# Expert weight loads: five instead of three outstanding, and chunks that are contiguous in DRAM

## The chip, the cores and the metric

The kernel runs as one program on one core of a Trainium2 chip. The metric is the device time of one execution in microseconds (us), as the median of several runs. The engines of the core that matter here are TensorE (PE), VectorE (DVE), ScalarE (ACT), GpSimd (POOL) and SyncE (SP, which issues most of the transfers), and the 16 DMA engines that all transfers share.

## The reference, cut to what matters

One layer of a streaming encoder runs over 1088 tokens (1024 of a prompt and 64 of a sample) with a model width of 1024. Attention, a short convolution and their merge come first. The part that the change touches is the mixture of experts behind them:

```python
def expert_block(args):          # 32 experts, hidden width 256; each token goes to 2 of them
    xblk, eid = args
    a = xblk @ w1[eid]           # 1024 -> 256
    b = xblk @ w3[eid]           # 1024 -> 256
    return (jax.nn.silu(a) * b) @ w2[eid]   # 256 -> 1024
```

The weighted outputs of a token's two experts are added to the residual. A last step adds `sigmoid(RMSNorm(x) @ w_pg) * (p @ w_ple)`. All inputs are float32. Each expert has 1024 x 512 weights in w1 and w3 together and 256 x 1024 in w2, so 3.146 MB; the 32 experts are 100.7 MB.

## The kernel before, in words

**Precision.** A product of float32 matrices is made of three matmuls (`mm3`, L60 to L63): each operand is split into a high part (`hi`, a cast on ACT, L55) and the rest (`lo`, a subtraction on DVE, L58). So each weight chunk that arrives in SBUF as `eraw` is first cast to `weh` on ACT and then subtracted to `wel` on DVE, before TensorE can use it. That pair is `e_split`.

**The order of the stages.** Projections, heads and attention; the merge with the output projection and the routing, token tile by token tile; the experts; then the combination of the experts' outputs with the gate (`f_comb`, `f_tr`, `f_mm`).

**The experts.** They run one after the other, e = 0 to 31. The rows of an expert's tokens (at most 96) are fetched from DRAM with an indirect transfer on POOL (`gather`, L1280, into one of three buffers `xg`), transposed on TensorE (`x_tr`), multiplied with w1 and w3 (`w13_mm`, 24 matmuls), passed through the activation (`act_`), transposed again (`a_tr`) and multiplied with w2 (`w2_mm`, 12 matmuls). The result `y` is copied out of PSUM by ACT (L1333) and written to the DRAM tensor `Yd` with another indirect transfer on POOL (`scatter`, L1336), which also ends the expert's work. The second product of expert e runs among the matmuls of expert e + 1.

**The weights.** An expert's weights are six chunks of [128, 1024] float32, 512 KB each (4 of w1 and w3, 2 of w2). `e_load` (L900) loads them into slots of SBUF; there are slots for five experts (`EP`), so the load for expert e + 5 waits until the chunk of expert e in the same slot has been split. The chunks of the first six experts are requested in the stages before the experts, among the loads and stores of the merge; from then on `late(e)` requests those of expert e + 6. SP's program order is written out by hand in these stages (`manual_schedule`), as is POOL's in the expert stage; the order on PE, ACT and DVE in the expert stage is made by the scheduler, from a model of times of its own.

**The bound on the queue.** Every load of weights goes through `w_dma` (L892 to L898): the load is given a dependency on the load issued three before it, so SP does not issue it before that one has landed:

```python
        r = eng.dma_start(dst, src)
        if len(wdma) >= 3:
            tc.add_manual_dep(r.ins, wdma[-3].name,
```

The same queue carries what the last step needs: five loads for `p @ w_ple` (`pl_load`, tiles `plr`) and eight of `w_pg` (`wpg_load`, tiles `eraw` from `in_wpg_dram`), which are requested after the last expert's chunks.

**The layout in DRAM.** The host packs the weights as `we` of shape [32, 128, 6144]: for each expert and each of the 128 partitions, 6 x 1024 numbers in a row. Chunk j of expert e is the slice `we[e, :, 1024 * j : 1024 * j + 1024]`: 128 pieces of 4 KB that lie 24 KB apart.

**After the experts.** A loop on the chip (`For_i`, L1524) serves tokens beyond an expert's first 96 rows; its count is worked out on the chip and no instruction of its body is in the trace of this input. All engines meet at it. Then SP loads the rows for the combination (`f_x`, `f_y`, L1572 and L1583; the latter read `Yd`, which the scatters wrote).

Of the kernel before, what the change touches and what calls it, by code (L numbers as in the profile page):

```python
# [32 lines left out]
NOV = 22  # L33
NOROW = 2200.0
A2 = 2 * T


@with_exitstack
def body(ctx, tc, a):
# [10 lines left out]
    def opened(*args, **kw):  # L50
        st = ExitStack()
        return st, st.enter_context(pool(*args, **kw))
# [17 lines left out]
    def load(p, shape, src, tag, bufs):  # L70
        raw = p.tile(shape, F32, name=tag + "_r", tag=tag + "_r", bufs=bufs)
        nc.sync.dma_start(raw, src)
        return raw
# [30 lines left out]
    h2d = dram.tile([T, D], F32, name="h2d")  # L104
    Yd = dram.tile([A2, D], F32, name="Yd")

    psA, pb = opened("pb", bufs=8, space=PSUM)

    def bank():
        return pb.tile([128, 512], F32, name="bk", tag="bk")  # L110
# [16 lines left out]

    ws, wp = opened("win", bufs=2, side="right")

# [1 line left out]
    wraw = {}  # L131
    wsp = {}

# [60 lines left out]
            lo(zTl[:, ct, o:o + n], zf[:, o:o + n], zTh[:, ct, o:o + n])  # L194
        return f

# [1 line left out]
    xs_, xp = opened("xin")  # L198
    nc.scalar.dma_start(ident, a["ident"])
    grow = xp.tile([1, D], F32, name="grow")  # L200
# [130 lines left out]
    jobs = [("b", 0, 2)]  # L331
# [28 lines left out]
    for j, (kind, d, g) in enumerate(jobs):  # L360
# [9 lines left out]
        for ci, (o, n) in enumerate([c for c in CH if c[0] < TB] if kind in "ag" else CH):  # L370
# [5 lines left out]
            if ci == 0:  # L376
# [3 lines left out]
                if j >= len(jobs) - 8:  # L380
                    k = j - (len(jobs) - 8)
                    r = load(gs_["qp"], [128, 544], a["wqkv"][:, k], "wq", 2)
# [8 lines left out]
    ws.close()  # L391
    zs.close()

# [1 line left out]
    lat, lp = opened("lat", side="right")  # L395
    kpe = lp.tile([32, NK], F32, name="kpe")
    gcol = lp.tile([64, 2], F32, name="gcol")
# [176 lines left out]
                                in1=rs[:, :, None].to_broadcast([128, NH, 64]), op=OP.mult)  # L574
        nc.sync.dma_start(knd[i // 4][:, :, i % 4].rearrange("q p c -> p q c"), kn.rearrange("p (q t) c -> p q (t c)", t=2))

# [1 line left out]
    FCH = [c for c in CH if c[0] >= TB]  # L578
    fw, fps, psF = {}, {}, []

# [44 lines left out]
    for nm, n, dst in (("wuq", 768, wu), ("wukv", 1024, wk)):  # L625
        for k in range(2):
            r = up.tile([128, 1024], F32, name="wup_r", tag="wup_r", bufs=1)
# [54 lines left out]
    fill_n(4)  # L682
    psA.close()

# [1 line left out]
    hws.close()  # L686
    us.close()
    lat.close()
# [149 lines left out]
    for u in range(-3, NU + 1):  # L838
        if 0 <= u < NU:
            u_T(u)  # L840
        if u + 3 < NU:
            h3, i3 = UN[u + 3]
            first = u == -3 or UN[u + 2][0] != h3
# [16 lines left out]
        o = u_PV(u - 1) if u >= 1 else None  # L860
# [8 lines left out]
    hbs.close()  # L869
    psS.close()  # L870

# [1 line left out]
    psB, pb = opened("pb2", bufs=7, space=PSUM)  # L873
    pst, ptab = opened("ptab", space=PSUM)
    tab = ptab.tile([128, 64], F32, name="tab")
# [3 lines left out]
    def slot(j, shape, dt, name):  # L879
        return (fx if j < 24 else fx2[0]).tile(shape, dt, name=name, tag=f"fx{j}", bufs=1)  # L880
# [9 lines left out]
    wdma = []  # L890

    def w_dma(dst, src, eng=nc.sync):  # L892
        r = eng.dma_start(dst, src)
        if len(wdma) >= 3:
            tc.add_manual_dep(r.ins, wdma[-3].name,
                              mybir.DependencyInfo(mybir.DependencyClass.Sync, mybir.DependencyReason.DATA),
                              reason="bounded queue")
        wdma.append(r.ins)  # L898

    def e_load(e, js=range(6)):  # L900
        for j in js:
            r = slot(3 * EP[e % len(EP)][j // 3] + j % 3, [128, 1024], F32, "eraw")
            w_dma(r, a["we"][e, :, 1024 * j:1024 * j + 1024])
            eraw[e, j] = r

    ys, yp = opened("ya", bufs=2)
# [35 lines left out]
    gates = lgp.tile([128, 2, NT], F32, name="gates")  # L942
# [155 lines left out]
        nc.vector.scalar_tensor_tensor(out=lg[:n, i], in0=ps[:n, 0:36], scalar=rs_.pop(i)[:n], in1=brt[:n],  # L1098
                                       op0=OP.mult, op1=OP.add)

# [1 line left out]
    V_ = nc.vector  # L1102
    gdesc, edesc, rid, ovn = c1[:, 0:4], c1[:, 4:12], c1[:, 12:140], c1[:, 140:140 + NOV]
    val, tok4 = c2[:, 0], c2[:, 1:5].rearrange("p (k s) t -> p k s t", k=2)
# [72 lines left out]
    for i in range(6):  # L1177
        p = i - 1
# [92 lines left out]
    V_.tensor_scalar(out=idx[:CAP].rearrange("p s e -> p (s e)"), in0=tab[:CAP], scalar1=NOROW, scalar2=None, op0=OP.add)  # L1271
    xs2.close()

# [1 line left out]
    xgs_, xgp = opened("xg")  # L1275
    xT, ab, act, aT2, yy = {}, {}, {}, {}, {}
    xgs = [xgp.tile([128, D], F32, name=f"xg{j}", bufs=1) for j in range(3)]
# [57 lines left out]
    def scatter(buf, col):  # L1335
        nc.gpsimd.indirect_dma_start(out=Yd[:, :], out_offset=bass.IndirectOffsetOnAxis(ap=col, axis=0), in_=buf,  # L1336
                                     in_offset=None, bounds_check=A2 - 1, oob_is_err=False)

# [5 lines left out]
    e_load(5)  # L1344
    order.close()

# [1 line left out]
    eps_, ep = opened("moe", bufs=2)  # L1348
    x_tr(0, xgs[0], 0, ep, CAP)
    x_tr(0, xgs[0], 1, ep, CAP)  # L1350
# [161 lines left out]
    eps_.close()  # L1512
    xgs_.close()

# [1 line left out]
    ops_, op_ = opened("ovf")  # L1516
    order = ExitStack()
    order.enter_context(tc.manual_schedule(engines={ET.DVE, ET.Activation, ET.SP}))
# [5 lines left out]
    with tc.For_i(0, nov, 1) as i:  # L1524
        ev = nc.values_load(ovi[0:1, bass.ds(i + 1, 1)], engines=(mybir.EngineType.SP,), min_val=0, max_val=NE - 1,
                            skip_runtime_bounds_check_because="bounded by a minimum on the chip")
        xgo = op_.tile([128, D], F32, name="xgo", tag="xyo")
        nc.gpsimd.memset(xgo, 0.0)
        rb = op_.tile([128, 128], F32, name="rb")
        V_.tensor_scalar(out=rb, in0=rid, scalar1=bs, scalar2=None, op0=OP.add)  # L1530
        V_.tensor_scalar(out=bs, in0=bs, scalar1=128.0, scalar2=None, op0=OP.add)
        ps = bank()
        for k in range(2):
            for t in range(NT):
                am = op_.tile([128, 128], F32, name="amo", bufs=1)
                V_.tensor_scalar(out=am, in0=rb, scalar1=slr[:, k, t:t + 1], scalar2=None, op0=OP.is_equal)
                nc.tensor.matmul(ps[:, 0:2], am, tok4[:, k, :, t], start=(k == 0 and t == 0),
                                 stop=(k == 1 and t == NT - 1))
        V_.tensor_scalar(out=gs, in0=ps[:, 0:2], scalar1=NOROW, scalar2=None, op0=OP.add)
        gather(xgo, gs[:, 0:1])  # L1540
        for b in range(2):
            x_tr("o", xgo, b, op_, 128)
        ab["o"] = bank()
        for k in range(KD):
            r = load(op_, [128, 512],
                     a["we"][bass.ds(ev, 1), :, 512 * k:512 * k + 512].rearrange("o p n -> p (o n)"), "ov", 1)
            wh, wl_ = split(op_, r, [128, 512], "ovs", 1)
            h, l = xT["o", k // 4]
            mm3(ab["o"], h[:, k % 4], l[:, k % 4], wh, wl_, k == 0, k == KD - 1)
        act_("o", op_, 128)  # L1550
        a_tr("o", op_, 128)
        yo = op_.tile([128, D], F32, name="yo", tag="xyo")
        h, l = aT2["o"]
        pso = [bank(), bank()]
        for j in range(2):
            for b in range(2):
                c = 4096 + 1024 * j + 512 * b
                r = load(op_, [128, 512], a["we"][bass.ds(ev, 1), :, c:c + 512].rearrange("o p n -> p (o n)"), "ov", 1)
                wh, wl_ = split(op_, r, [128, 512], "ovs", 1)
                mm3(pso[b], h[:, j], l[:, j], wh, wl_, j == 0, j == 1)  # L1560
        for b in range(2):
            nc.scalar.copy(yo[:, 512 * b:512 * b + 512], pso[b])
        scatter(yo, gs[:, 1:2])
# [7 lines left out]
        r0, n = 128 * i, TN[i]  # L1571
        nc.sync.dma_start(XY[i][0][:n], x1d[r0:r0 + n])  # L1572

# [1 line left out]
    fs, fp = opened("tail", bufs=1)  # L1575
    hT3 = [[fp.tile([128, KD, 128], F32R, name=f"hT3{n}") for n in "hl"],
           [wpx_get(q).rearrange("p (k n) -> p k n", k=KD) for q in (4, 5)]]
# [98 lines left out]
def pack(inp):  # L1676
    import numpy as np
    f = lambda n: np.asarray(inp[n])
    A = {}
# [4 lines left out]
    groups = []  # L1684
# [24 lines left out]
    A["wr"] = kp(np.concatenate([f("w_rg")[0], f("w_re")[0]], 1))  # L1709
    w13 = np.concatenate([f("w1")[0], f("w3")[0]], 2).reshape(32, 8, 128, 512).transpose(0, 2, 1, 3)  # L1710
    w2 = f("w2")[0].reshape(32, 2, 128, 1024).transpose(0, 2, 1, 3)
    A["we"] = np.concatenate([w13.reshape(32, 128, 4096), w2.reshape(32, 128, 2048)], 2)
    A["wpg"] = kp(f("w_pg")[0])
    A["wple"] = kp(f("w_ple")[0])
    p = np.concatenate([f("p_prompt")[0, 0], f("p_sample")[0, 0]], 0)
# [65 lines left out]
```

## Time and profile before

| what | value |
|---|---|
| median of 3 runs | 1382.01 us (1380.19 to 1383.79) |
| span of the profiled execution, first to last instruction | 1379.2 us |
| TensorE matmul busy | 1276.2 us, 93% of the span |
| VectorE, ScalarE busy | 851.5 us (62%), 653.1 us (47%) |
| moved by all DMA queues | 272.36 MB, 197 GB/s on average |
| loads of expert weights | 192 of 512 KB |

The profiled execution has no time of its own beside its span; the span lies 2.8 us under the median of the runs. The page divides the span into 40 slices of 34.5 us, in tenths of busy time; the granted clock of TensorE and the share of the DMA engines stand under them in the same slices. Views by window and timeline give microseconds from the start of the span. A row of waits names the engine and line that waited, what ended the wait, the total in us, how often, and the longest.

### The profile page before, as it was taken

The page shows a single profiled execution, that of the slowest core. Times are in us where ns is not written, and L with a number is a line of the kernel's source. Part 1 is how long each engine was busy: PE and PEld are TensorE (multiplying, and loading weights), DVE is VectorE, ACT ScalarE, POOL GpSimd, SP SyncE. Part 2 cuts the span into 40 slices and gives each one's busy share as a digit, 9 for nine tenths or more (in the row PEclk, how much of TensorE's full clock was granted, in tenths as well). Part 3 has the DMA queues.
Part 4 walks back from the last instruction along what each step waited for, and adds up shares of the span by engine and source line. Part 5 has one row for each costly group of instructions (what it writes and reads, how often), then busy time and mean ns, then how long its engine had stood idle before and what let it go on. Part 6 is the DMA issues. An engine that isn't in the chain of part 4 may idle for free. (4 is left out here: it accounts for less than half of the span.)

```text
span 1379.2 us, 20412 instructions
## 1 busy us (share of the span) xinstructions
PE 1276.2 (93%) x7235; PEld 1102.1 (80%) x7235; DVE 851.5 (62%) x1627; ACT 653.1 (47%) x1276; POOL 327.1 (24%) x375
## 2 busy tenths in 40 slices
PE   7999999999989999999999999299999887988998
PEld 6999999989879888889998887176666655657886
DVE  7333343236674566766488555698889766875743
ACT  6221232223444455565454121288888665776422
POOL 2000011125553233343144000422222221200210
PEclk9999999999999999999999999599999999999999
DMA  5111398553575423323287657679999999988511
GB/s 193 62 46 47 110 372 296 210 163 102 151 239 162 157 85 127 117 72 99 87 288 250 233 210 256 194 233 310 301 307 292 299 300 304 308 289 311 216 48 54
DMA packets 106057, 272.36 MB, mean 197 GB/s; under 512 B 13521, under 2 KB 42689, under 8 KB 105922
## 3 DMA queue, kind: packets, MB, share of 16 engines
q1 hardware_dynamic: 89968, 220.29, 47.2%
q0 software_dynamic: 15840, 50.68, 11.6%
q8 instruction: 58, 0.95, 0.3%
q14 instruction: 45, 0.37, 0.1%
q10 hardware_dynamic: 146, 0.07, 0.0%
HBM read 211.14 MB, written 67.19 MB: 202 GB/s over the span
## 5 line engine op out<-in xcount | busy, mean ns | idle before, releaser
L58 DVE TENSOR_TENSOR wel<-eraw,weh 128x1024 fp32r<-128x1024 f32 x190 | 227.8, 1222 | 59.1 <-ACT weh L55 56.2
L55 ACT CAST weh<-eraw 128x1024 fp32r<-128x1024 f32 x192 | 197.6, 1054 | 40.6 <-DMA eraw<-in_we_dram 27.4
L61 PE MATMUL bk<-weh,xTh 128*96 128x512 f32 x256 | 104.9, 410 | 7.2 <-ACT xTh L55 4.5
L62 PE MATMUL bk<-wel,xTh 128*96 128x512 f32 x256 | 105.3, 411 | 3.3 <-DVE wel L58 3.3
L768 POOL TENSOR_TENSOR P<-P,ri 128x128 f32<-128x128 f32 (+8 forms) x72 | 77.3, 1079 | 128.2 <-DVE ri L767 108.5
L63 PE MATMUL bk<-weh,xTl 128*96 128x512 f32 x256 | 104.4, 408 | 0.1
L1336 POOL DMA_INDIRECT Yd<-y,idx x32 | 40.6, 1267 | 256.6 <-ACT y L1333 228.3
L58 DVE TENSOR_TENSOR wl<-w_r,wh 128x1024 fp32r<-128x1024 f32 x28 | 34.3, 1225 | 77.4 <-ACT wh L55 77.0
L61 PE MATMUL bk<-hTAh,wh 128*128 128x384 f32 x224 | 75.6, 337 | 0.8 <-ACT hTAh L55 0.8
L62 PE MATMUL bk<-hTAl,wh 128*128 128x384 f32 x224 | 75.6, 337 | 0.3 <-DVE hTAl L58 0.3
L63 PE MATMUL bk<-hTAh,wl 128*128 128x384 f32 x224 | 75.3, 336 | 0.0
L61 PE MATMUL fg<-hTBh,fw 128*128 128x384 f32 (+1 forms) x224 | 74.5, 332 | 0.3 <-ACT fgm L604 0.2
L55 ACT CAST wh<-w_r 128x1024 fp32r<-128x1024 f32 x28 | 29.5, 1053 | 93.8 <-PE bk L62 88.4
L63 PE MATMUL fg<-hTBh,fw 128*128 128x384 f32 (+1 forms) x224 | 72.9, 326 | 0.0
L62 PE MATMUL fg<-hTBl,fw 128*128 128x384 f32 (+1 forms) x224 | 72.7, 324 | 0.0
L61 PE MATMUL bk<-weh,ath 128*96 128x512 f32 x128 | 52.4, 409 | 19.4 <-ACT ath L55 19.4
L61 PEld LDWEIGHTS bk<-weh,xTh 128*96 128x96 f32 x256 | 42.4, 166 | 27.5 <-ACT xTh L55 7.1
L62 PE MATMUL bk<-hTBl,wh 128*128 128x384 f32 (+1 forms) x192 | 62.1, 324 | 0.3 <-DVE hTBl L58 0.3
L61 PE MATMUL bk<-hTBh,wh 128*128 128x384 f32 (+1 forms) x192 | 62.2, 324 | 0.0
L63 PE MATMUL bk<-hTBh,wl 128*128 128x384 f32 (+1 forms) x192 | 61.8, 323 | 0.0
L62 PEld LDWEIGHTS bk<-wel,xTh 128*96 128x96 f32 x256 | 42.4, 166 | 24.1 <-DVE wel L58 9.7
L754 DVE TENSOR_REDUCE nm<-S 128x1 f32<-128x128 f32 (+8 forms) x72 | 50.8, 706 | 12.4 <-PE S L63 11.3
(782 smaller groups left out, 3761.4 us busy)
## 6 DMA issues: line engine op xcount, KB each, us to landing
eraw<-in_we_dram SPq DMA_DIRECT2D x192, 512.0 KB, 5.7
fw<-wsd POOLq DMA_DIRECT2D x32, 512.0 KB, 5.0
w_r<-in_wing_dram SPq DMA_DIRECT2D x28, 512.0 KB, 5.3
gm_r<-gscr SPq DMA_DIRECT2D x16, 544.0 KB, 4.5
wsd<-wh SPq DMA_DIRECT2D x16, 512.0 KB, 3.8
wsd<-wl SPq DMA_DIRECT2D x16, 512.0 KB, 4.4
xy<-Yd SPq DMA_DIRECT2D x16, 512.0 KB, 9.8
vd<-V SPq DMA_DIRECT2D x10, 512.0 KB, 4.1
```

The lines of the kernel that those rows point to most:

```text
L55: nc.scalar.copy(dst, src)
L58: (eng or nc.vector).tensor_tensor(out=dst, in0=src, in1=h.bitcast(F32), op=OP.subtract)
L61: r = nc.tensor.matmul(ps, sh, mh, start=first, stop=False)
L62: nc.tensor.matmul(ps, sh, ml, start=False, stop=False)
L63: nc.tensor.matmul(ps, sl, mh, start=False, stop=last)
L754: nc.vector.tensor_reduce(out=nm, in_=s, axis=AX.XY, op=OP.max, negate=True)
L768: nc.gpsimd.tensor_tensor(out=P[:, :nk], in0=P[:, :nk], in1=ri.to_broadcast([128, nk]), op=OP.mult)
L1336: nc.gpsimd.indirect_dma_start(out=Yd[:, :], out_offset=bass.IndirectOffsetOnAxis(ap=col, axis=0), in_=buf, in_offset=None, bounds_check=A ...
```

## The change

`w_dma` now makes a load depend on the load issued five before it (`DEEP = 5`), and the host packs the weights as `we` of shape [32, 6, 128, 1024], so that each chunk is one contiguous piece of 512 KB. The loop for overflowing tokens reads the same numbers from the new places. Comments on stages were dropped, so line numbers differ by one or more.

```diff
+DEEP = 5
...
     def w_dma(dst, src, eng=nc.sync):
         r = eng.dma_start(dst, src)
-        if len(wdma) >= 3:
-            tc.add_manual_dep(r.ins, wdma[-3].name,
+        if len(wdma) >= DEEP:
+            tc.add_manual_dep(r.ins, wdma[-DEEP].name,
                               mybir.DependencyInfo(mybir.DependencyClass.Sync, mybir.DependencyReason.DATA),
                               reason="bounded queue")
         wdma.append(r.ins)
...
             r = slot(3 * EP[e % len(EP)][j // 3] + j % 3, [128, 1024], F32, "eraw")
-            w_dma(r, a["we"][e, :, 1024 * j:1024 * j + 1024])
+            w_dma(r, a["we"][e, j])
...
-    A["we"] = np.concatenate([w13.reshape(32, 128, 4096), w2.reshape(32, 128, 2048)], 2)
+    we = np.concatenate([w13.reshape(32, 128, 4096), w2.reshape(32, 128, 2048)], 2)
+    A["we"] = np.ascontiguousarray(we.reshape(32, 128, 6, 1024).transpose(0, 2, 1, 3))
```

**SP, in the middle of the expert stage.** Each row is the load of one chunk; the bracket names the semaphores it waits for. The loads complete on eight semaphores DMAHW0 to DMAHW7 in turn; the DVE semaphore is the slot's, given back by the split of the chunk that lay there. Before:

```order
L893 DMA eraw_11027<-in_we_dram 128x1024 [waits DMAHW7_49,DVE_49]
L893 DMA eraw_11029<-in_we_dram 128x1024 [waits DMAHW0_49,DVE_49]
L893 DMA eraw_11031<-in_we_dram 128x1024 [waits DMAHW1_49,DVE_49]
L893 DMA eraw_11033<-in_we_dram 128x1024 [waits DMAHW2_49,DVE_49]
L893 DMA eraw_11035<-in_we_dram 128x1024 [waits DMAHW3_49,DVE_49]
```

Now:

```order
L894 DMA eraw_11027<-in_we_dram 128x1024 [waits DMAHW5_49,DVE_49]
L894 DMA eraw_11029<-in_we_dram 128x1024 [waits DMAHW6_49,DVE_49]
L894 DMA eraw_11031<-in_we_dram 128x1024 [waits DMAHW7_49,DVE_49]
L894 DMA eraw_11033<-in_we_dram 128x1024 [waits DMAHW0_49,DVE_49]
L894 DMA eraw_11035<-in_we_dram 128x1024 [waits DMAHW1_49,DVE_49]
```

The loads stand in the same order; each waits for the semaphore two places earlier in the turn, and still for its slot.

**PE, expert 27.** In these rows `bk_12724` is the sum of w1 and w3 of expert 27, `bk_12745` and `bk_12753` are the two halves of the second product of expert 26 (from `ath`, `atl`), and the matmuls from `xg1` transpose the rows of expert 28. Before:

```order
L61 MATMUL bk_12724<-weh_12671,xTh1_12691 96x512
L61 MATMUL bk_12745<-weh_12563,ath_12734 96x512
L62 MATMUL bk_12745<-wel_12564,ath_12734 96x512
L61 MATMUL bk_12753<-weh_12563,ath_12734 96x512
L62 MATMUL bk_12753<-wel_12564,ath_12734 96x512
L1290 MATMUL bk_12774<-ident_58,xg1_9636 128x96 x4
L1290 MATMUL bk_12803<-ident_58,xg1_9636 128x96 x4
L62 MATMUL bk_12724<-wel_12672,xTh1_12691 96x512
```

Now:

```order
L62 MATMUL bk_12724<-weh_12671,xTh1_12691 96x512
L63 MATMUL bk_12724<-wel_12672,xTh1_12691 96x512
L64 MATMUL bk_12724<-weh_12671,xTl1_12692 96x512
L62 MATMUL bk_12724<-weh_12671,xTh1_12691 96x512
L63 MATMUL bk_12724<-wel_12672,xTh1_12691 96x512
L64 MATMUL bk_12724<-weh_12671,xTl1_12692 96x512
L62 MATMUL bk_12745<-weh_12563,ath_12734 96x512
L63 MATMUL bk_12745<-wel_12564,ath_12734 96x512
L62 MATMUL bk_12753<-weh_12563,ath_12734 96x512
L63 MATMUL bk_12753<-wel_12564,ath_12734 96x512
L1291 MATMUL bk_12774<-ident_58,xg1_9636 128x96 x4
L1291 MATMUL bk_12803<-ident_58,xg1_9636 128x96 x4
```

The last matmuls of expert 27's first product stood behind the second product of expert 26; now they stand ahead of it. Up to this place PE, ACT and DVE have the same order in both kernels, all through experts 0 to 26; from here to expert 31 pieces of the same work change places.

## Rows read from the trace of the kernel before

**Rows 1.** The page: busy time, and the 40 slices of the span.

```profile
span 1379.2 us, 20412 instructions
...
PE 1276.2 (93%) x7235; PEld 1102.1 (80%) x7235; DVE 851.5 (62%) x1627; ACT 653.1 (47%) x1276; POOL 327.1 (24%) x375
...
PEclk9999999999999999999999999599999999999999
DMA  5111398553575423323287657679999999988511
```

**Rows 2.** Busy time by window: length, engines (instructions), PEclk, DMA share, GB/s.

```profile
core 0: us, PE busy (x) PEld busy (x) DVE busy (x) ACT busy (x) POOL busy (x), PEclk, DMA share, GB/s
...
920.00:1076.00 156.00, 150.30 (x740) 105.18 (x738) 136.67 (x161) 130.39 (x192) 39.42 (x32) 1.00 0.93 303
1080.00:1220.00 140.00, 118.32 (x531) 80.20 (x530) 100.01 (x116) 95.14 (x138) 27.39 (x22) 0.93 0.92 301
...
1260.00:1280.00 20.00, 20.00 (x97) 16.56 (x96) 11.94 (x13) 12.58 (x20) 1.51 (x4) 1.00 1.02 406
```

**Rows 3.** Timeline of POOL: a scatter ends each expert; every fourth and the last.

```profile
start us, us, engine line op out<-in xcount [idle before <-releaser]
915.66 1.33 POOL L1336 DMA_INDIRECT Yd<-y,idx  x1 [7.72 <-ACT y L1333]
...
955.12 1.31 POOL L1336 DMA_INDIRECT Yd<-y,idx  x1 [9.61 <-ACT y L1333]
...
994.11 1.31 POOL L1336 DMA_INDIRECT Yd<-y,idx  x1 [9.61 <-ACT y L1333]
...
1059.74 1.32 POOL L1336 DMA_INDIRECT Yd<-y,idx  x1 [5.95 <-ACT y L1333]
...
1072.12 1.32 POOL L1336 DMA_INDIRECT Yd<-y,idx  x1 [9.61 <-ACT y L1333]
...
1244.10 1.16 POOL L1336 DMA_INDIRECT Yd<-y,idx  x1 [7.62 <-DMA Yd<-y,idx]
```

**Rows 4.** Waits of ACT, 1068 to 1245 us.

```profile
ACT weh L55 <- DMA eraw<-in_we_dram: 27.4, 26, 3.2
...
ACT plh L55 <- DMA plr<-in_wple_dram: 2.4, 2, 1.8
...
ACT weh L1238 <- DMA eraw<-in_wpg_dram: 1.3, 1, 1.3
```

**Rows 5.** Waits of SP's queue, 1068 to 1226 us.

```profile
SPq L893 <- DMA eraw<-in_we_dram: 127.5, 78, 4.8
SPq L893 <- DVE wel L58: 1.6, 5, 0.4
```

**Rows 6.** Transfers from 901 to 1225 us: packets, MB, share; issues, median us to landing.

```profile
q1 hardware_dynamic: 22133, 80.62, 76.0%
q0 software_dynamic: 6384, 15.63, 15.4%
...
eraw<-in_we_dram SPq DMA_DIRECT2D x156, 512.0 KB, 6.1
Yd<-y,idx POOLq DMA_INDIRECT x29, 6.0
xg<-h2d,idx POOLq DMA_INDIRECT x28, 8.4
```

**Rows 7.** Timeline of SP from 896 us: the first load of expert 6.

```profile
901.63 9.63 SPq L893 DMA_DIRECT2D eraw<-in_we_dram  x6
```

**Rows 8.** The tile eraw: all its loads, duration in ns, first and last start.

```profile
L893 SPq DMA_DIRECT2D eraw<-in_we_dram x192: 327/328/1233, 746.4 to 1224.7; - x192
```

**Rows 9.** Timeline of ACT: the last three casts of expert 15.

```profile
1041.88 2.96 ACT L55 CAST weh<-eraw 128x1024 fp32r<-128x1024 f32 x3
```

**Rows 10.** Timeline of ACT: the last cast of expert 31.

```profile
1230.51 1.05 ACT L55 CAST weh<-eraw 128x1024 fp32r<-128x1024 f32 x1 [0.23 <-DMA eraw<-in_we_dram]
```

**Rows 11.** Transfers in the merge stage, 760 to 860 us: packets, MB, share.

```profile
q1 hardware_dynamic: 6432, 23.33, 66.4%
```

**Rows 12.** Waits of PE, 740 to 896 us: the longest, for expert 0's rows.

```profile
PE bk L1290 <- DMA xg<-h2d,idx: 14.9, 1, 14.9
```

More of the change, by code (lines that the diff above doesn't have):

```diff
@@ L1545, in body @@
             r = load(op_, [128, 512],
-                     a["we"][bass.ds(ev, 1), :, 512 * k:512 * k + 512].rearrange("o p n -> p (o n)"), "ov", 1)
+                     a["we"][bass.ds(ev, 1), k // 2, :, 512 * (k % 2):512 * (k % 2) + 512].rearrange("o p n -> p (o n)"),
+                     "ov", 1)
             wh, wl_ = split(op_, r, [128, 512], "ovs", 1)
@@ L1556, in body @@
             for b in range(2):
-                c = 4096 + 1024 * j + 512 * b
-                r = load(op_, [128, 512], a["we"][bass.ds(ev, 1), :, c:c + 512].rearrange("o p n -> p (o n)"), "ov", 1)
+                c = slice(512 * b, 512 * b + 512)
+                r = load(op_, [128, 512], a["we"][bass.ds(ev, 1), 4 + j, :, c].rearrange("o p n -> p (o n)"), "ov", 1)
                 wh, wl_ = split(op_, r, [128, 512], "ovs", 1)
```

## The prediction

> **What bounds the kernel now.** I read the page first. TensorE is busy 93% of the span [rows 1], so a transfer can matter only where TensorE has gaps. The line of the granted clock shows one deep dip, where the routing ends and the experts begin; the DMA line stands at nine tenths from just behind that dip until shortly before the end [rows 1]. That stretch is the expert stage, and the change touches its loads alone.
>
> The windows split the stage in two [rows 2]. From 920 to 1076 us TensorE runs 740 matmuls in 156 us, 4.74 per us. From 1080 to 1220 us it runs 531 in 140 us, 3.79 per us, and its clock falls to 0.93. The transfers are the same in both halves: 303 and 301 GB/s at a DMA share of 0.93 and 0.92. So the first half lives on the six experts that were loaded ahead, and in the second that store is used up and TensorE follows the transfers. The scatters show the pace per expert [rows 3]. The scatter of expert 0 starts at 915.66 us, those of experts 4 and 8 at 955.12 and 994.11, that of expert 16 at 1072.12: 39.0 us for four experts, 9.75 each. Expert 31 follows at 1244.10: 15 experts in 172.0 us, 11.47 each. Four experts of 39.0 us repeat without a change, so with weights at hand expert 31 (the same place in the group of four as expert 15, at 1059.74) would scatter at 1059.74 + 4 x 39.0 = 1215.7 us. **The lateness of the weights therefore costs 1244.1 - 1215.7 = 28.4 us.** The windows agree: at 4.74 per us the 531 matmuls need 112 us of the 140, 28 us less.
>
> What makes the weights late? ACT waits 27.4 us in 26 waits for a chunk [rows 4]. SP, which could ask for them earlier, waits 127.5 us for the load three before and only 1.6 us for a slot given back by a split [rows 5]. The bound on the queue is what holds the loads, not the slots. Three loads of 0.524 MB that land after 6.1 us in the median [rows 6] are one load every 2.03 us; the 156 loads from expert 6 on start between 901.63 [rows 7] and 1224.7 us [rows 8], one every 323.1 / 155 = 2.084 us. The two agree, so the rate is what three outstanding give.
>
> **The change part by part.** *Five outstanding.* No transfer and no instruction is added. SP's order stays; each load's wait moves two loads back, so the load itself, and all that stands behind it on SP, goes out earlier. What the rate becomes must be bounded. From below: no better than now, 2.084 us per load. From above: the last window moves 406 GB/s at a share of 1.02 [rows 2], 398 at a full share. Nearer is the stage itself: 80.62 + 15.63 = 96.25 MB in 324 us at 76.0 + 15.4 = 91.4% [rows 6] are 325 GB/s at a full share. The merge stage, which loads expert chunks by the old layout among stores, gives 23.33 MB / (0.664 x 100 us) = 351 GB/s [rows 11].
>
> With the gathers and scatters, a chunk comes with 96.25 / 156 = 0.617 MB. At 325 GB/s that is 1.90 us per load. The last one then goes out at 901.63 + 155 x 1.90 = 1196.1 us, lands five intervals later at 1205.6, and its cast ends 1.05 us behind that, at 1206.7. Before, that cast ended at 1230.51 + 1.05 = 1231.6 [rows 10], so 24.9 us are saved. At 351 GB/s it is 1.76 us, and the chunk lands at 901.63 + 160 x 1.76 = 1183 us; but at the undisturbed pace ACT casts it only by 1041.88 + 2.96 + 156 = 1200.8 us [rows 9]. So the transfers stop mattering and the full 28.4 us are saved. The line between the two is 901.63 + 160 x i = 1199.8, i = 1.86 us or 331 GB/s, close to the stage's own value. I take 27 us: between the two results, nearer the upper, because part of the slow packets now are the first ones behind an empty queue.
>
> *What is late next.* With five outstanding the loads run ahead until the five experts' slots are full, and SP waits for a split instead; then the 9.75 us of an expert are the floor. I cost nothing below it: TensorE is busy 150.3 of 156 us there, DVE 136.7, ACT 130.4 [rows 2].
>
> *The contiguous chunk.* It moves the same bytes into the same 128 partitions. From below, nothing: 325 GB/s as above. From above, 398 GB/s, the window whose loads read whole rows of DRAM that follow each other. Either is above or within 2% of the 331 that suffices, so I add nothing to the sum.
>
> *The tail.* The loads for `p @ w_ple` and `w_pg` stand behind the last chunks in the same queue, and come earlier with them. ACT waits 2.4 and 1.3 us for them [rows 4], so the gain lies between 0 and 3.7 us. The meeting of the engines behind the experts also needs the last scatter, which waited 7.62 us for the scatter before [rows 3]; so I take 2.
>
> *The order of experts 27 to 31* changes with the scheduler's model of the queue. It is the same work; a piece that stood behind the second product of expert 26 now stands ahead of it, as in most experts before. Nothing, within 2 us either way.
>
> *Before the experts*, TensorE waits 14.9 us for expert 0's rows [rows 12], beside loads of expert 5 that wait for slots in either version. Nothing; at best 14.9 - 8.4 = 6.5 us (an undisturbed gather, [rows 6]), at worst about one more load each for two more outstanding, 2 x 2.0 = 4 us.
>
> **The sum:** 27 + 2 = 29 us off the 1379.2 us of the profiled execution is 1350.2. The median of the runs lies 2.8 us above that execution's span, so I expect **1353.0 us**.
>
> **The rivals.** *The queue is already full* (no change). The DMA share of 0.93 says that the engines have little idle time. Then five outstanding only land later, 5 x 2.08 = 10.4 us instead of 6.1, and the interval stays: 1382 us. Against it: the same engines move 398 GB/s at a full share elsewhere, and even the stage's own value leaves 8% of a share. A milder form is likelier: at 310 GB/s the interval is 1.99, the last chunk lands at 901.63 + 160 x 1.99 = 1220, is cast by 1221, and with 1 us of tail 1382 - 10.5 - 1 = 1370.5 us. The Trainium skill, "DMA: Bandwidth & Descriptors", in its section on the anatomy of one DMA, fits a transfer issued by GpSimd with about 2 us plus its bytes at 436 GB/s. By that fit, as an estimate, a chunk takes 3.2 us and three outstanding already overlap the fixed part, so that more of them would bring nothing: 1382 us. The trace differs: 6.1 us to landing, and 2.08 us per load where the fit's data part is 1.2.
>
> *Gathers starve behind the deeper queue* (slower). Rows of expert e + 3 are fetched into the buffer that expert e has left, so a landing may take about two experts, 20 us, before TensorE waits; it takes 8.4 now [rows 6]. Above that, three experts last as long as a landing and one expert, (L + 9.75) / 3 each. The break-even with today's mean of 10.6 us (328.4 us for 31 experts, [rows 3]) is L = 22 us. At L = 27 an expert takes 12.25 us and 31 take 380: 51 us more, 1433 us. For it speaks only that two more chunks stand in line; against it, that the gathers come by a queue of their own and would have to become 2.6 times as slow. The Trainium skill, same page, section on queues, rings and completion order, says that a DMA engine goes round the queues packet by packet; by that rule the depth of one queue takes no turns from another. No row here shows a deeper queue, so I leave this rival a small chance.
>
> *The chunks' packets get faster as well* (faster still). With 398 GB/s everywhere the floor of 9.75 us remains; with the whole tail the result is 1382 - 28.4 - 3.7 = 1350 us, inside the range.
>
> *The change doesn't do what it says*: if slots hold the loads, depth is idle. The 1.6 us of waits for a split [rows 5] exclude that for the second half.
>
> **How the numbers follow.** The forecast and its faster variant together get 0.80, the milder form of the full queue 0.12, no change 0.05, slower 0.03. The lower end takes the full 28.4, a tail of 3.7 and some of the 6.5 us ahead of the experts: 1345. The upper end, 1368, is the milder form at 312 GB/s; beyond it lie about 2 in 10 with the low side. A measurement of this kernel can tell about 0.3% (4 us) from no change; faster by more than that gets 0.92, within it 0.05, slower 0.03.
>
> **What would show it.** Right: the scatters keep 39.0 us for four experts up to the last, which starts near 1216 to 1218 us; SP's waits for the load before shrink and waits for a split appear; landing rises to 8 to 10 us while the stage moves over 320 GB/s; ACT's 27.4 us of waits go to a few. Wrong: landing rises to 10 us at 300 GB/s (queue full), or TensorE waits for gathered rows in the middle of the stage (starved).

## The result, and the profile after

The changed kernel takes **1350.11 us** in the median of four runs (1349.19 to 1351.81). The kernel before took 1381.82 us in the four runs beside it (1380.19 to 1383.79). The ratio is 0.9767, with a 95% interval of 0.9739 to 0.9795: the change is faster by 2.3%. The forecast was 1353.0 us, in a range of 1345 to 1368. The profiled execution took 1351.81 us; its span is 1349.8 us, 29.4 less than the 1379.2 of before [rows 1]. It was the slowest of its four, so the spans differ by less than the medians do (31.7 us).

The page of the changed kernel (line numbers behind the new constant are one higher than before):

```profile
span 1349.8 us, 20413 instructions
...
PE 1268.6 (94%) x7235; PEld 1100.1 (81%) x7235; DVE 848.0 (63%) x1627; ACT 649.7 (48%) x1276; POOL 323.8 (24%) x375
...
PEclk9999999999998999999999999869999999999999
DMA  5111298734477523242257656769999999967511
```

Against [rows 1] TensorE is busy 7.6 us less, the others within 3.5 us. So 21.8 of the 29.4 us are idle time of TensorE that went; the same number of matmuls also ran a little shorter, at a clock that no longer falls in the stage. Busy time by window (length, then busy time of each engine with its instructions, granted clock, share of the DMA engines, GB/s):

```profile
core 0: us, PE busy (x) PEld busy (x) DVE busy (x) ACT busy (x) POOL busy (x), PEclk, DMA share, GB/s
920.00:1076.00 156.00, 150.30 (x738) 105.12 (x737) 136.58 (x161) 130.05 (x192) 38.71 (x32) 1.00 0.99 350
1080.00:1180.00 100.00, 97.15 (x477) 68.09 (x475) 87.82 (x104) 84.41 (x126) 25.95 (x21) 1.00 1.01 346
```

The first half runs as before, 738 matmuls in 156 us [rows 2], while the transfers move 350 GB/s instead of 303 beside them. The second half, which ran 3.79 matmuls per us at a clock of 0.93, now runs 4.77 at full clock. The scatters, from the timeline of POOL, those of experts 0, 4, 10, 16, 20, 24, 25, 28, 30 and 31:

```profile
start us, us, engine line op out<-in xcount [idle before <-releaser]
917.07 1.33 POOL L1337 DMA_INDIRECT Yd<-y,idx  x1 [10.01 <-ACT y L1334]
...
956.55 1.32 POOL L1337 DMA_INDIRECT Yd<-y,idx  x1 [9.64 <-ACT y L1334]
...
1013.46 1.31 POOL L1337 DMA_INDIRECT Yd<-y,idx  x1 [5.98 <-ACT y L1334]
...
1073.58 1.31 POOL L1337 DMA_INDIRECT Yd<-y,idx  x1 [9.64 <-ACT y L1334]
...
1112.60 1.31 POOL L1337 DMA_INDIRECT Yd<-y,idx  x1 [9.64 <-ACT y L1334]
...
1151.60 1.32 POOL L1337 DMA_INDIRECT Yd<-y,idx  x1 [9.61 <-ACT y L1334]
1160.74 1.31 POOL L1337 DMA_INDIRECT Yd<-y,idx  x1 [6.37 <-ACT y L1334]
...
1187.98 0.93 POOL L1337 DMA_INDIRECT Yd<-y,idx  x1 [8.46 <-ACT y L1334]
...
1207.61 0.92 POOL L1337 DMA_INDIRECT Yd<-y,idx  x1 [7.28 <-ACT y L1334]
1213.55 1.26 POOL L1337 DMA_INDIRECT Yd<-y,idx  x1 [5.01 <-ACT y L1334]
```

Experts 16, 20 and 24 scatter 39.02 and 39.00 us apart, the step of the undisturbed first half in [rows 3]. Before, the last scatter started at 1244.10 us; now it starts at 1213.55.

The change also brought another order of the engines' work, but only from experts 26 and 27 on. The scatter of expert 25 comes ahead of that place. Before:

```profile
1182.21 1.31 POOL L1336 DMA_INDIRECT Yd<-y,idx  x1 [6.39 <-ACT y L1333]
```

That was 266.6 us behind the scatter of expert 0; now it is 1160.74 - 917.07 = 243.7 us. So 22.9 of the 32.0 us that the stage became shorter, from the first scatter to the last, were gained while TensorE, ACT and DVE ran the same order as before. The other 9.1 us lie in the six experts whose order changed too.

ACT's waits for chunks (1068 to 1215 us), then SP's waits (1068 to 1226 us):

```profile
ACT weh L56 <- DMA eraw<-in_we_dram: 1.0, 1, 1.0
```

```profile
SPq L894 <- DMA eraw<-in_we_dram: 93.4, 67, 3.1
SPq L894 <- DVE wel L59: 5.8, 17, 0.7
```

ACT's 27.4 us in 26 waits [rows 4] are down to one of 1.0 us, and a gap of that length at the same place four experts later (1135.07 us) is put down to a matmul, so that even this one may be no wait for a chunk. SP's 127.5 us of waits for an earlier load [rows 5] are 93.4, but the last load also goes out earlier: it is 81% of the 156.7 us from 1068 to the last load before, and 83% of 112.5 us now. Slots hold SP for only 5.8 us. The first load of expert 6 in SP's timeline, and the tile of all loads (duration of the issue in ns, first and last start):

```profile
903.33 2.26 SPq L894 DMA_DIRECT2D eraw<-in_we_dram  x2
```

```profile
L894 SPq DMA_DIRECT2D eraw<-in_we_dram x192: 327/328/1234, 750.7 to 1180.5; - x192
```

The 156 loads from expert 6 on lie (1180.5 - 903.3) / 155 = **1.788 us** apart, against 2.084 before. The transfers of that stretch, 901 to 1196 us:

```profile
DMA packets 30077, 101.17 MB, mean 343 GB/s; under 512 B 5443, under 2 KB 5443, under 8 KB 30055
q1 hardware_dynamic: 23619, 85.11, 82.1%
q0 software_dynamic: 6436, 15.78, 16.0%
...
Yd<-y,idx POOLq DMA_INDIRECT x29, 7.0
xg<-h2d,idx POOLq DMA_INDIRECT x28, 8.6
```

The two queues together hold the DMA engines for 98.1% of the time (91.4% in [rows 6]) and move 343 GB/s. Gathers land after 8.6 us, as before (8.4); scatters take 7.0 instead of 6.0.

### The profile page after: what moved, and what is told of

The parts are those of the page before. It is cut to its first block, busy times and chain, and to the rows that moved or that the text cites. A ratio compares the mean times of both kernels' runs of the same rounds, so it can differ in the third digit from the quotient of the medians.

```text
span 1349.8 us, 20413 instructions
## 1 busy us (share of the span) xinstructions
PE 1268.6 (94%) x7235; PEld 1100.1 (81%) x7235; DVE 848.0 (63%) x1627; ACT 649.7 (48%) x1276; POOL 323.8 (24%) x375
## 5 line engine op out<-in xcount | busy, mean ns | idle before, releaser
L56 ACT CAST weh<-eraw 128x1024 fp32r<-128x1024 f32 x192 | 196.0, 1054 | 11.7 <-PE bk L64 10.7
L59 DVE TENSOR_TENSOR wl<-w_r,wh 128x1024 fp32r<-128x1024 f32 x28 | 34.3, 1225 | 75.7 <-ACT wh L56 75.3
L56 ACT CAST wh<-w_r 128x1024 fp32r<-128x1024 f32 x28 | 29.4, 1050 | 91.8 <-PE bk L63 86.3
```

The lines of the kernel that those rows point to most:

```text
L56: nc.scalar.copy(dst, src)
L59: (eng or nc.vector).tensor_tensor(out=dst, in0=src, in1=h.bitcast(F32), op=OP.subtract)
```

## The experiments

The forecast had held. Open was which of the two parts did it, what lies beyond five, and what sets the floor. Each ratio is against runs of the kernel before on the same chip.

### Either part alone

The theory: depth does it all, since rate is what outstanding loads give. The rival: the layout makes the packets shorter and has a share.

`e1_depth_only` is the kernel before, with the depth alone:

```diff
-        if len(wdma) >= 3:
-            tc.add_manual_dep(r.ins, wdma[-3].name,
+        if len(wdma) >= 5:
+            tc.add_manual_dep(r.ins, wdma[-5].name,
```

> Five outstanding loads with the old layout, chunks of 4-KB pieces that lie 24 KB apart. Theory 'depth': the number outstanding sets the rate, the layout nothing; the loads from expert 6 on start every 1.79 us as with the change, the last expert scatters near 1214 us, the time is 1350 us within 3. Rival 'layout': contiguous chunks make the packets faster and depth only lengthens the landing; the loads stay at 2.08 us apart and the time at 1382 us. Both in part: an interval between 1.85 and 2.0 us and 1355 to 1372 us.

Measured: 1349.89 us (1346.43 to 1351.99), ratio 0.9765 (0.9735 to 0.9794). That is the result of the whole change. On TensorE, ACT and DVE the expert stage has the order of the changed kernel, row for row. Its transfers from 901 to 1180 us, and its tile of loads (the first load of expert 6 starts at 899.07 us):

```profile
q1 hardware_dynamic: 22465, 81.81, 82.5%
q0 software_dynamic: 6259, 15.32, 16.4%
...
eraw<-in_we_dram SPq DMA_DIRECT2D x155, 512.0 KB, 8.9
```

```profile
L893 SPq DMA_DIRECT2D eraw<-in_we_dram x192: 327/328/1233, 746.8 to 1174.5; - x192
```

The interval is (1174.5 - 899.1) / 155 = 1.777 us at 98.9% share, and a chunk lands after 8.9 us, where 6.1 stood for three.

`e2_layout_only` is the changed kernel with the old depth:

```diff
-DEEP = 5
+DEEP = 3
```

> Three outstanding loads with the new, contiguous layout. Theory 'depth': nothing changes, 2.08 us per load and 1382 us within 4. Rival 'layout': the loads come every 1.79 us and the time is 1350 us. Both in part: in between, with an interval under 2.0 us.

Measured: 1375.75 us (1372.74 to 1377.35), ratio 0.9938 (0.9918 to 0.9959). On the three engines its expert stage has the order of the kernel before. The same views as for e1:

```profile
q1 hardware_dynamic: 19003, 69.23, 75.0%
q0 software_dynamic: 5707, 13.93, 15.7%
...
eraw<-in_we_dram SPq DMA_DIRECT2D x134, 512.0 KB, 6.1
```

```profile
L894 SPq DMA_DIRECT2D eraw<-in_we_dram x192: 327/328/1233, 749.2 to 1221.4; - x192
```

Loads start every (1221.4 - 903.1) / 155 = 2.053 us instead of 2.084; over 155 loads that is 4.8 us of the 7.9 between the medians (1383.61 before, on that chip); the rest is not accounted for. So the contiguous chunk is worth about 0.6% as long as three are outstanding, and nothing that the intervals of e1 and of the change can separate at five. Depth is the change: by itself up to expert 25 (22.9 us, above), and from there with the order that it brings.

### Four and seven outstanding

`e3_deep4` and `e4_deep7` are the changed kernel with `DEEP = 4` and `DEEP = 7`.

> Four outstanding, contiguous chunks. Theory 'depth, with matmuls as the floor': the interval lies between 2.08 and 1.79, near 1.90 us; the last load then starts near 901.6 + 155 x 1.90 = 1196 us and lands by 1204, when its cast would be due near 1201 to 1203, so the time is 1350 to 1355 us, nearly all of the gain. Rival 'every outstanding load counts alike': half of the gain, 1366 us.

Four: 1354.08 us (1353.65 to 1355.66), ratio 0.9792 (0.9765 to 0.9819). Its tile of loads:

```profile
L894 SPq DMA_DIRECT2D eraw<-in_we_dram x192: 327/328/1330, 749.1 to 1187.9; - x192
```

Loads start every (1187.9 - 902.3) / 155 = 1.843 us and land after 7.6. The forecast had put the line at which weights stop being late at 1.86 us. At 1.843 ACT waits for no chunk from 1068 to 1217 us, so the line held; still the kernel is 4 us behind five. To the scatter of expert 25 it takes 243.6 us, as five does (243.7); 3.0 us are lost behind it, where its order is another.

> Seven outstanding, contiguous chunks. Theory 'depth, with matmuls as the floor': the loads come a little faster still (the DMA share is 0.98 to 0.99 with five, so 1.75 to 1.79 us per load) and the time stays at 1350 us within 4, but for what the scheduler's other order of the expert stage costs. Rival 'transfers still bound': it falls by 5 us or more, to 1345 or under. Rival 'gathers starve': landing of the gathers goes from 8.6 to over 15 us, TensorE waits for gathered rows, and the time is above 1355.

Seven: 1394.04 us (1393.48 to 1394.76), ratio 1.0078 (1.0051 to 1.0106): **slower than before**, and 44 us slower than five. Neither theory had that. The waits of its TensorE, 896 to 1300 us, those of its SP, 901 to 1260, and a window of its stage with the columns shown above:

```profile
PE bk L62 <- ACT xTh L56: 20.6, 16, 2.4
...
PE bk L62 <- ACT ath L56: 8.6, 7, 2.7
...
PE bk L63 <- DVE wel L59: 1.0, 2, 0.8
```

```profile
SPq L894 <- DVE wel L59: 142.9, 91, 16.0
SPq L894 <- DMA eraw<-in_we_dram: 79.6, 63, 3.2
```

```profile
1080.00:1120.00 40.00, 32.79 (x134) 21.76 (x133) 25.95 (x30) 23.91 (x35) 7.38 (x6) 0.87 0.87 279
```

The weights aren't late here. SP waits for slots, the last load goes out at 1185.7 us, and expert 31 starts at 1236.6, 51 us behind it. The gathers land after 8.3 us, so they don't starve either. TensorE waits 20.6 us for its transposed rows, and its clock falls to 0.87 in that window. From 1016 us on, in the first product of expert 12, the scheduler has put the instructions of TensorE, ACT and DVE in another order than for five. Up to there the order is the same. Two scatters ahead of that place, and the loads from 901 to 1180 us with their time to landing:

```profile
917.35 1.33 POOL L1337 DMA_INDIRECT Yd<-y,idx  x1 [9.02 <-ACT y L1334]
...
1013.71 1.31 POOL L1337 DMA_INDIRECT Yd<-y,idx  x1 [5.98 <-ACT y L1334]
```

```profile
eraw<-in_we_dram SPq DMA_DIRECT2D x154, 512.0 KB, 9.7
```

From the scatter of expert 0 to that of expert 10 it takes 96.4 us, as with five (1013.46 - 917.07). In that stretch the queue is at its fullest: from 901 to 1013 us the same view gives 65 loads that land after 11.4 us. That is one load every 1.7 us, so between six and seven are under way at a time. So loads that deep cost nothing as long as the order stays. Behind that place, from 1035 to 1185 us, they land after only 7.6 us, and there the stage loses its 47 us (247.2 from expert 10 to expert 31, where five takes 200.1). A piece of the other order, with five and then with seven (W: first product of an expert, a and x: transposes, Y: second product of the expert before, each with its number of matmuls):

```
five:   W19x13 a18x2 W19x11 Y18x4 x20x8 Y18x8
seven:  W19x2 a18x2 W19x12 Y18x4 W19x4 Y18x8 W19x6 x20x8
```

With seven, the transposes of the next expert's rows stand at the very end of an expert instead of inside the second product. The first product of the next expert then waits for their copies. These experts take up to 14.0 us from first product to first product, where five has 9.2 to 11.1.

### The order of the engines written out by hand

Is it the order that costs those 44 us, or the seven loads? A second way to ask is to give each depth the same order over the whole stage. First attempt, `e5_fixed3`, `e6_fixed5` and `e7_fixed7`: the loop of the experts sets the order on all five engines, with the casts of a chunk and the activation where I thought right, at depths 3, 5 and 7. Part of the edit:

```diff
-    order.enter_context(tc.manual_schedule(engines={ET.Pool, ET.SP}))
+    order.enter_context(tc.manual_schedule(engines={ET.PE, ET.DVE, ET.Activation, ET.Pool, ET.SP}))
...
-        sp = [(nx, j) for j in range(6)] if nx < NE else []
+        if nx < NE:
+            sp = [(e, 4), (e, 5)] * (e >= 1) + [(nx, j) for j in range(4)]
```

> The order of the expert stage on all engines is written out by hand and is the same in this and the next two runs; three outstanding, contiguous chunks. Theory 'transfers bound at three': 2.05 us per load as in the run with the new layout alone, the last expert late by the transfers, 1370 to 1380 us. Rival 'the order made by the scheduler was what held three outstanding back': it is as fast as the same order with five, within 4 us.

> The same written-out order, five outstanding. Theory 'depth gives the rate, the order gives the floor': 1.79 us per load; if the order costs 9.4 to 9.8 us per expert the time is 1340 to 1352 us.

> The same written-out order, seven outstanding. Theory 'the loss with seven was the scheduler's order': with the order fixed the time is that of five, within 4 us, or a little less. Rival 'seven outstanding itself costs (transfers, gathers, or engines kept from SBUF)': it is slower than five with the same order by 10 us or more, toward the 44 us seen with the scheduler's order.

Measured: 1497.01, 1498.18 and 1498.59 us, ratios 1.0838 (1.0793 to 1.0883), 1.0835 (1.0787 to 1.0884) and 1.0842 (1.08 to 1.0884). The times that were expected with three and five were missed by over 100 us: my order is 8% poorer than the scheduler's. That seven takes the time of five came out as expected, and so did the rival for three, that it is as fast as five, but for another reason than the ones given. ACT's longest wait in the one with five, 960 to 1300 us:

```profile
ACT y L1334 <- PE bk L64: 106.3, 48, 4.8
```

ACT stands at the copy of `y` while the casts behind it wait, and an expert takes about 14.3 us. An order that slow hides the loads at any depth, so these runs say only that depth is worth nothing where the weights aren't late.

`e8_fixed5_light` is e6 with less TensorE work, to see what the floor is made of:

```diff
-            mm3(ab[e][:n], h[:, k % 4, 0:n], l[:, k % 4, 0:n], wh[:, c], wl_[:, c], k == 0, k == KD - 1)
+            mm2(ab[e][:n], h[:, k % 4, 0:n], wh[:, c], wl_[:, c], k == 0, k == KD - 1)
```

> The written-out order with five outstanding, and the first product of each expert leaves out the matmuls of the low part of the rows with the high part of the weights (8 of 24 matmuls, 1.9 us of TensorE per expert), so that TensorE is no longer the floor. Theory 'transfers are next, a store of five experts ahead': the last load still starts near 1180 us, its cast follows by 1190, and the time falls by some 8 to 14 us against the same order with all matmuls. Rival 'TensorE alone is the bound with five': it falls by 25 us or more, up to 31 x 1.9 = 59.

Measured: 1480.14 us (1478.36 to 1483.68), ratio 1.0713 (1.0669 to 1.0757), 18 us less than e6. That lies between the two expectations, in an order that binds by itself: inconclusive. The 1.9 us were too small as well: a matmul of the first product takes 0.40 us by the changed kernel's page, so eight are 3.2 us.

Second attempt, `e9_pe_fixed3`, `e10_pe_fixed5` and `e11_pe_fixed7`: the changed kernel with TensorE's order alone added to what the loop writes out, ACT and DVE left to the scheduler.

```diff
-    order.enter_context(tc.manual_schedule(engines={ET.Pool, ET.SP}))
+    order.enter_context(tc.manual_schedule(engines={ET.PE, ET.Pool, ET.SP}))
```

> The order of TensorE in the expert stage is the one in which the loop is written, the same in this and the next two runs; ACT and DVE are still ordered by the scheduler (nearly alike with three, the same with five and seven). Three outstanding, contiguous chunks. Theory 'transfers bound at three': the loads stay at 2.05 us apart and the time at 1370 to 1380 us, whatever pace this order could hold. Rival 'the scheduler's order was the limit at three': the time is that of the next run.

> The same TensorE order, five outstanding. Theory 'depth gives the rate, the order the floor': the loads come every 1.79 us; the last one then starts near 1180 us and lands by 1190. If this order holds 9.3 to 9.5 us per expert, without the wait of 1.4 us for a transposed activation in every fourth, the last expert starts near 1188 to 1193 and the time is 1338 to 1347 us, faster than the change. If it holds no better pace than 9.75, it is 1350 us or more.

> The same orders on TensorE, ACT and DVE as with five, seven outstanding. Theory 'the loss with seven was the scheduler's order': the time is that of five within 4 us. Rival 'seven outstanding itself costs': it is slower than five with the same order by 10 us or more, and TensorE or ACT waits for gathered rows, chunks or transfers.

Measured: 1412.2 us (ratio 1.0192, 1.0154 to 1.0229), 1393.89 (1.0071, 1.0051 to 1.0091) and 1394.05 (1.0065, 1.0041 to 1.0089). For five and seven the orders on TensorE, ACT and DVE are the same row for row, and so is the time within 0.2 us. **With this order a bound of seven costs nothing against a bound of five.** For three neither expectation held: it takes longer than 1370 to 1380 us, and is not as fast as five. TensorE's longest wait in e10, 920 to 1260 us, and SP's, 901 to 1260:

```profile
PE bk L1317 <- DVE sa L1310: 45.3, 31, 2.6
```

```profile
SPq L894 <- DVE wel L59: 175.9, 108, 15.1
```

Here TensorE comes to the transposes of the activation 1.5 us before they are ready, once per expert, and an expert takes 10.75 us up to expert 28. SP waits for slots, with seven as well, and so the queue is never seven deep. The loads of e11 from 901 to 1180 us:

```profile
eraw<-in_we_dram SPq DMA_DIRECT2D x155, 512.0 KB, 6.6
```

They land after 6.6 us, those of e10 after 6.4, far from the 11.4 of e4's first experts. So it is e4's first part, and not this pair, that clears seven outstanding loads themselves. **Both together leave the order as what cost the 44 us of e4**; no run repeats e4's order at another depth.

Three outstanding fall behind by 18 us, and the same view of TensorE's waits says by which wait of e9:

```profile
PE bk L1317 <- DVE sa L1310: 42.9, 30, 2.6
PE bk L62 <- ACT ath L56: 16.9, 1, 16.9
```

One wait of 16.9 us near the end is nearly all of it; up to there ACT's order is that of e10. ACT stands then at the cast of a load for `p @ w_ple`, which comes through the same queue behind the last chunks, as its waits from 920 to 1290 us say:

```profile
ACT plh L56 <- DMA plr<-in_pT_dram: 17.6, 1, 17.6
```
The last chunk itself had gone out at 1212.0 us, before expert 31 started at 1253.4.

### What the stage waits for next

`e12_deep5_light` makes the edit of e8 in the changed kernel, so that the scheduler sets the order.

> What the stage waits for next, with five outstanding: the first product leaves out the matmuls of the low part of the rows with the high part of the weights (8 of 24 per expert), so the output differs in the last bits; about 3.2 us per expert less on TensorE, with the weights, the splits and the transfers untouched. If the transfers are next (six loads at 1.79 us are 10.7 us per expert, more than the 9.75 us of the floor, so that the store of six experts is nearly used up at the end): the last load is issued at 1178 to 1183 us as before, its cast ends near 1190, the last scatter starts 11 us behind it, near 1201, and the kernel takes 1336 to 1342 us, 8 to 14 us less than with all matmuls; ACT's waits for a chunk come back. If transfers have room (the loads are held by slots alone): DVE with 8.5 us per expert is next, 31 experts save about 39 us, the last load goes out before 1165 us, and the kernel takes 1305 to 1318 us.

Measured: 1360.98 us (1352.4 to 1361.19), ratio 0.9833 (0.9774 to 0.9892): 11 us *more* than with all matmuls (9 by the two ratios, which compare each with the kernel before on its own chip), outside both expectations. The loads did as the theory of the transfers had it. Its tile of loads, and SP's waits from 901 to 1178 us:

```profile
L894 SPq DMA_DIRECT2D eraw<-in_we_dram x192: 327/328/1233, 749.7 to 1177.4; - x192
```

```profile
SPq L894 <- DMA eraw<-in_we_dram: 183.0, 135, 3.2
SPq L894 <- DVE wel L59: 27.2, 30, 13.8
```

With the first load of expert 6 at 902.66 us the interval is (1177.4 - 902.7) / 155 = 1.772 us, and SP waits for loads, not for slots: less work on TensorE doesn't bring the weights faster. But expert 31 starts only at 1205.2 us, 28 us behind the last load, and the last scatter at 1222.26. TensorE is busy 82 of the 100 us from 1080 to 1180, at a clock of 0.90. Its longest wait from 1080 to 1222 us is for casts by ACT (first row), and ACT's longest is for TensorE's products (second):

```profile
PE bk L68 <- ACT weh L56: 10.7, 8, 2.5
```

```profile
ACT y L1334 <- PE bk L64: 13.4, 15, 2.6
```

The chunks were there by then: ACT's waits from 900 to 1222 us name none, where the theory had them come back. So the loss lies in how the engines follow each other; that the scheduler's order is its cause was not tested, and what a stage with less TensorE work and a good order would take remains open.

## Why the prediction was right, point by point

**The lateness of the weights costs 28.4 us.** Right. From the first scatter to the last it was 1244.10 - 915.66 = 328.4 us and is 1213.55 - 917.07 = 296.5. The 32.0 us between them are the 28.4 and 3.6 more. The pattern of the first half would have put the last scatter at 917.07 + 144.1 + 4 x 39.0 = 1217.2 us (144.1 from expert 0 to expert 15 in [rows 3]). It came 3.6 earlier, since experts 28 to 31 took 35.3 us from scatter to scatter (1178.21, the scatter of expert 27, to 1213.55) instead of 39.0. By [rows 3] alone the 28.4 us are a reckoning from the pace; the 22.9 us gained up to expert 25 show the larger part of them under an unchanged order.

**The rate.** The taken 27 us of 28.4 stood for an interval a little above 1.86 us; it is 1.788, or 1.777 in e1. The bracket of 325 to 351 GB/s at a full share holds the measured 343 / 0.981 = 350, at its upper end. The step that was too cautious is "between the two results". Its reason points the right way: with depth alone the packets did get faster, for e1 reaches 349 / 0.989 = 353 with the old layout, where three had 325. That the slow ones were those behind an empty queue is not shown by any run.

**What is late next.** This step was wrong in its mechanism, though not in its number. "The loads run ahead until the five experts' slots are full, and SP waits for a split instead" did not happen: SP waits 93.4 us for loads and 5.8 for slots. Six loads at 1.788 us are 10.7 us per expert, still more than the 9.75 of the floor, so the store of six experts goes on being eaten up. It only lasts to the end: the last load goes out at 1180.5 us and expert 31 starts at 1196.9, 16.4 us later (4-deep: 11.8). Before, it had started 1.1 us ahead of the last load. What counts is the chunk in SBUF: with the 8.9 us of e1 it lands near 1189.4, and its cast starts at 1202.6, 13 us later (with four, 1187.9 + 7.6 and 1204.3: 9 us). So what the kernel has is a reserve at the last expert, and not a queue with room: at 10.73 - 9.75 = 0.98 us per expert, some 13 experts more would have used it up (an estimate from these numbers).

**The contiguous chunk adds nothing.** Right at five (e1). At three it is worth 0.6%, which the step allowed: the loads come 1.5% faster (2.053 us for 2.084), and that counts only where the rate is short.

**The tail, 2 us.** Wrong by 3.2. From the last scatter to the end it was 1379.2 - 1244.1 = 135.1 us and is 136.3. ACT's waits for `plr` and for `w_pg` [rows 4] are gone as forecast, but the meeting of the engines still stands 10.3 us behind the last scatter (SP's next load at 1254.35 before, at 1223.84 now). In both traces that load comes 0.2 to 0.3 us behind the end of ACT's last instruction ahead of the meeting (a cast of `w_pg` that ends at 1254.11 before, a copy of a `p @ w_ple` product that ends at 1223.50 now), while the last scatter of before had landed at 1250.5. So ACT's work beside the scatter seems to hold the meeting, and not the scatter, as the step reasoned; no run tests that. With the other terms the misses cancel: 32.0 - 1.4 (a stage that began later) - 1.2 is the 29.4 us that the span lost, where the sum said 29. That agreement to 0.4 us is luck: the stage gave 5 us more than the 27 of the sum, and the tail and the start took them back.

**The order of experts 27 to 31, "nothing, within 2 us".** Against the pattern of 39.0 us the last four experts gained 3.6 us, more than the step allowed. How much of that is the order is not shown. Expert 31 has no next expert's matmuls behind it in any order, and its scatter comes 5.9 us behind the one before, where the pattern has 8.7. But e3, whose order parts from that of five at the same place and whose ACT waits for no chunk, is 3.0 us longer there, so an order can be worth that much. It is the least founded step. With seven (e4) the same scheduler makes an order with which the kernel is 44 us slower. None of the rivals was an order that the new depth brings with it, and in e4 such an order cost more than the change gains.

**The rivals.** *The queue is full*: at three it was not, since four and five raise the rate from 2.05 to 1.84 and 1.78 us per load. At five it is, at 98% share. The fit in the Trainium skill ("DMA: Bandwidth & Descriptors", on the anatomy of one DMA) is one for transfers issued by GpSimd; taken for these loads, as the prediction's estimate did, it would have had three already saturate. The runs differ: they show 297 to 303 GB/s with three, 334 with four and 343 to 349 with five. *Gathers starve*: 8.4 us became 8.6, and 8.3 in e4, so the gathers did not suffer; the scatters take 1 us longer, to no effect. The Trainium skill, on the same page (section on queues, rings and completion order), has each DMA engine go round the queues packet by packet. The gathers agree with that; the longer scatters are not explained.

## What to carry to other kernels

A bound on outstanding transfers is a rate: depth divided by time to landing, where the time to landing grows with the depth (6.1 us at three, 8.9 at five). Compare the interval that it gives with the pace of the consumer, and if the transfers are slower, work out at which unit the store that was loaded ahead runs out; only that unit's deadline decides. And where a scheduler sets the order, a change of depth changes the order too: compare the orders before you credit or blame the queue, and tell them apart by the stretch in which the orders still agree, or by a run that holds one fixed. Such a run says something of the depth only if the queue in it is as deep as allowed: the time to landing shows it.

## What the runs showed of the hardware that was not expected

- Time to landing grows with depth, but more slowly than depth: 6.1 us with three loads of 512 KB outstanding (e2), 7.6 with four, 8.9 with five (e1), 11.4 with seven allowed (e4, 901 to 1013 us). The first three are depth times interval (3 x 2.05, 4 x 1.84, 5 x 1.78), to within 4%, and from four to five the interval falls by only 3% (1.843 to 1.788).
- Two kernels with the same loads and the same work differ by 44 us (e4 and the change); what parts them is the order of the engines. TensorE's granted clock falls to 0.87 in a stretch of e4 in which it is busy for 32.8 of 40 us, where the changed kernel keeps 1.00 at 97.15 of 100 us.
- Pieces of 4 KB that lie 24 KB apart and pieces that follow each other load at nearly the same rate: 2.084 against 2.053 us per load at three outstanding, 1.777 against 1.788 at five.
